# In-place sigmoids in PSUM, and the stores of c11 and p4 on SP's queue, in a one-core decoder layer

## The chip, the cores and the metric

The kernel runs on one core of one Trainium2 chip. The metric is the device time of one execution in microseconds (us); the number to beat or to meet is the median of 3 runs of the kernel before, 2428.19 us (2426.36 to 2428.45). The engines are PE (TensorE, the matmuls), DVE (VectorE), ACT (ScalarE), POOL (GpSimd) and SP (SyncE, which here does nothing but issue DMA transfers). Each engine works through its own list of instructions in a fixed order, and semaphores hold an instruction until what it needs is there.

## The reference

One decoder layer over 2048 tokens of width 1024: a normalised input is projected once to a convolution branch (512 channels, gated, 31 taps) and to eight attention heads of 64; both branches share one output projection; then comes a SwiGLU block. The part that the change touches is the attention, which has no softmax. For a query t and the keys s before it:

```
z = q . k / 8
A[t, s] = sigmoid(z[t, s]) * product over s < j < t of (1 - sigmoid(z[t, j]))
out[t] = sum over s of A[t, s] * v[s]
```

Since 1 - sigmoid(z) = sigmoid(-z), the product is a running product of sigmoid(-z), taken from the newest key back to the oldest. If R[t, s] is the product over j from s to t-1, then A[t, s] = R[t, s+1] - R[t, s], so the kernel never forms A: it multiplies R by differences of neighbouring rows of v (the tile `step`), and adds v once at the end.

## The kernel before, in words

All products run in float32r with both operands split into a high and a low part (H and L): a product is three matmuls, L.H, H.H and H.L, summed in one PSUM bank. ACT makes H by copying with rounding, DVE or POOL makes L by a subtraction.

The work is cut into four groups g of 512 tokens. For each group there are stages on PE, in the order of the table `PLAN`: `in` (input projection, matmuls into `inps`), `mixc` and `outc` (output projection of the convolution half), `mixa` and `outa` (of the attention half), and for the SwiGLU block `fprep`, `c11` and `p4`. The SwiGLU block uses a seven-product scheme in place of eight, on half matrices; `c11` and `p4` are two of its terms that are computed ahead of the rest and kept in DRAM until the later loop `five` reads them. Beside these stages three side tasks run: the attention (`attn`), the convolution taps on DVE (`taps`, L824) and sums of weight halves on POOL (`sums`).

The attention walks over units (head, key chunk of 512). A unit has four `scores`, one for each block of 128 queries, and four `values`. A score is: two matmuls into a PSUM tile `z` (L908, L909), of which there are two; a sigmoid on ACT from `z` into an SBUF tile `om` (L911), of which there are eight; and a scan on DVE, a running product along the keys from right to left. The scan works in place on `om`. There are three forms of it:

- the diagonal chunk (c == g, L914): `lower`, an SBUF tile with a single one per row, is the first input and `om` the second; the widths are 128, 256, 384 and 512 for the four blocks;
- the other chunks (L916): `om` is the first input, and the second, which the operation ignores, is a broadcast of one column, `z[:, 0:1]` in PSUM;
- the same for the last group's heads 4 to 7, where `late` is true: the ignored input is `one`, in SBUF.

So `z` is in use until the sigmoid has read it (diagonal and late scores), or until the scan has finished (the others). `values` then transposes `om` on PE (L934 into `at`), splits it (ACT L590 into `TH`, DVE L591 into `TL`) and multiplies (L939, L940 into `o`).

The results of `c11` (88 tiles of 128 x 512) go from PSUM by ACT (L1146) into four quarters of one SBUF tile, taken in turn, and those of `p4` (22 tiles) by ACT (L1175) into one of four buffers. Each is then stored by `store` (L1109), whose DMA is issued by ACT's own queue (`eng=nc.scalar`, L1147 and L1176; the trace puts the issue at L1111). All other DMAs are issued by SP.

The order of the instructions up to the end of the attention is not the order of the code. A planner inside the kernel (`Graph`, `cost`) takes the recorded instructions, gives each a price, simulates the engines and the buffers, and writes the resulting order on every engine. A DMA costs the queue that issues it 450 ns in that plan; a DVE scan costs 2.04 ns per element and 240 ns more, or 125 ns more where one of its operands lies in PSUM. When the code changes, this plan is made anew.

Of the kernel before, what the change touches and what calls it, by code (L numbers as in the profile page):

```python
# [13 lines left out]
AF = mybir.ActivationFunctionType  # L14
ALU = mybir.AluOpType
# [4 lines left out]
P = 128  # L20
# [5 lines left out]
NH = 8  # L26
# [3 lines left out]
G = 512  # L30
NG = S // G
# [448 lines left out]
def layer_kernel(ctx: ExitStack, tc: tile.TileContext, x, xT, g_pre_mix, w_in, conv_w, conv_b, ln_g, ln_b,  # L480
                 attn_g, w_out, g_post_mix, g_pre_ffn, w_gate, w_up, w_down, g_post_ffn, out):
    nc = tc.nc
# [31 lines left out]
    def bank(name):  # L514
        return mm.tile([P, G], F32, tag="mm", name=name)

    def ev(name, dt=F32, n=G):
        return rp.tile([P, n], dt, tag="ev", name=name, bufs=4)
# [53 lines left out]
    class Weights:  # L572
# [9 lines left out]
        def next(self):  # L582
            while len(self.tiles) < min(self.n + 1 + self.ahead, len(self.srcs)):
                self.tiles.append(self.load(self.srcs[len(self.tiles)]))
            self.n += 1
            return self.tiles[self.n - 1]
# [49 lines left out]
    lower = ap.tile([P, G], F32, name="lower", bufs=1)  # L636
# [5 lines left out]
    one = cc.tile([P, 1], F32, name="one")  # L642
# [3 lines left out]
    for c in range(CB):  # L646
        t = vp.tile([P, PAD + G], F32, name=f"glu{c}")
# [231 lines left out]
    def attn(g):  # L879
# [13 lines left out]
        def fetch(h, c):  # L893
            K = ap.tile([P, G], F32R, tag="K", name="K")
            V = ap.tile([P, G], F32R, tag="V", name="V")
            nc.sync.dma_start(K.bitcast(F32), kd[h, c].bitcast(F32))
            nc.sync.dma_start(V.bitcast(F32), vd[h // 2, c][:, h % 2, :].bitcast(F32))
            return dict(h=h, c=c, K=K, V=V, A=[])

        def scores(u, j):  # L900
            hd_ = heads[u["h"]]
            diag = u["c"] == g
            w = (j + 1) * P if diag else G
            K = u["K"]
            z = pp.tile([P, G], F32, tag="z", name="z")
            late = g == NG - 1 and u["h"] >= NH // 2
            js = slice(j * P, (j + 1) * P)
            nc.tensor.matmul(z[:, 0:w], hd_["QL"][:, js], K[:, 0:w], start=True, stop=False)  # L908
            nc.tensor.matmul(z[:, 0:w], hd_["QH"][:, js], K[:, 0:w], start=False, stop=True)  # L909
            om = ap.tile([P, G], F32, tag="om", name="om", bufs=NOM)  # L910
            nc.scalar.activation(om[:, 0:w], z[:, 0:w], AF.Sigmoid, scale=-0.125)  # L911
            r = om[:, 0:w][:, ::-1]
            if diag:
                nc.vector.tensor_tensor_scan(r, lower[:, G - w:G][:, ::-1], r, hd_["prev"][j], ALU.add, ALU.mult)  # L914
            else:
                nc.vector.tensor_tensor_scan(r, r, (one if late else z[:, 0:1]).to_broadcast([P, w]), hd_["prev"][j],  # L916
                                             ALU.mult, ALU.bypass)
            hd_["prev"][j] = om[:, 0:1]
            if w == P and g:
                hd_["prev"][j] = sp.tile([P, 1], F32, tag="pv", name="pv", bufs=2)  # L920
                nc.gpsimd.tensor_tensor(hd_["prev"][j], om[:, 0:1], lower[:, G - P - 1:G - P], ALU.add)
            u["A"].append(om)
            return w
# [56 lines left out]
        for n in range(len(units) + 1):  # L980
            u = None
            if n < len(units):
                h, c = units[n]
# [3 lines left out]
                u = fetch(h, c)  # L987
            for i in range(TT):
                w = 0
# [11 lines left out]
            if last is not None and last["c"] == 0:  # L1001
                h = last["h"]
                oT = ap.tile([P, G], F32, tag="oT", name="oT", bufs=1)
                nc.scalar.activation(oT, heads[h]["o"], AF.Copy)
                if h % 2 == 0:
                    vsh = ap.tile([P, G], F32, tag="vsh", name="vsh", bufs=1)
                    n = int(g == 0)
# [95 lines left out]
    def matmul(ps, a, b, **flags):  # L1103

        return nc.tensor.matmul(ps, a, b, skip_group_check=True, **flags)  # L1105

    stored = {}

    def store(t, *key, eng=nc.sync):  # L1109
        stored[key] = dp.tile([P, *t.shape[1:]], F32, name="_".join(str(k) for k in key))  # L1110
        eng.dma_start(stored[key], t)  # L1111

    def part(t, k, n, *key, eng=nc.sync):

        if key not in stored:
            stored[key] = dp.tile([P, n, G], F32, name="_".join(str(k) for k in key))
        eng.dma_start(stored[key][:, k, :], t)

    fx = {}

# [9 lines left out]
    def c11(g):  # L1130

        Hs, Ls = fx[g]
        t = cm.tile([P, 2, D], F32, tag="big", name="c11", bufs=2)
        cs = cycle([t[:, i // 2, i % 2 * G:(i % 2 + 1) * G] for i in range(4)])
        wts = Weights([(w, j) for j in range(HF) for w in W], 1)
        for j in range(HF):
            ws = [wts.next() for _ in W]
            pss = [bank("c11") for _ in W]
            for hf in range(2):
                for i, ((WH, WL), ps) in enumerate(zip(ws, pss)):  # L1140
                    for k in range(4):
                        kc = slice((4 * hf + k) * P, (4 * hf + k + 1) * P)
                        for a, b, last in ((WL, Hs, False), (WH, Hs, False), (WH, Ls, k == 3)):
                            matmul(ps, a[:, kc], b[hf][:, k, :], start=hf == k == 0 and a is WL, stop=last)
                    c = next(cs)
                    nc.scalar.activation(c, ps, AF.Copy)  # L1146
                    store(c, "c11", g, i, j, hf, eng=nc.scalar)  # L1147
                    yield 0.5

    def sums_split(HL, k, t, eng=nc.gpsimd):  # L1150
# [4 lines left out]
    def sum_in(g, n, H, L, eng=nc.vector):  # L1155
        for k in range(4):
            t = ev("sumin")
            nc.sync.dma_start(t, stored["B", g, n][:, k, :])
            sums_split((H, L), k, t, eng)

    def p4(g):

        Hs, Ls = ([xp.tile([P, 4, G], F32R, tag=tag, name=tag, bufs=2)] for tag in ("xH", "xL"))
        sum_in(g, 4, Hs[0], Ls[0])
        wts = Weights([(w, j + HF) for j in range(HF) for w in W], load=half_w)
        for j in range(HF):
            for i in range(2):
                WH, WL = wts.next()
                ps = bank("p4")
                for k in range(4):  # L1170
                    kc = slice(k * P, (k + 1) * P)
                    for a, b, last in ((WL, Hs, False), (WH, Hs, False), (WH, Ls, k == 3)):
                        matmul(ps, a[:, kc], b[0][:, k, :], start=k == 0 and a is WL, stop=last)
                c = ev("p4")
                nc.scalar.activation(c, ps, AF.Copy)  # L1175
                store(c, "p4", g, i, j, eng=nc.scalar)  # L1176
                yield 1

    def sums():
# [12 lines left out]
        def flush(n):  # L1192
            while len(late) > n:
                t, kind, *key, m = late.pop(0)
                if kind == "S":
                    ns = (6, 7) if m in (6, 7) else (5, 3)
                    part(t, ns.index(m), 2, kind, *key, ns)
                else:
                    store(t, kind, *key, m)
# [96 lines left out]
    for name, g, cost, *mid in PLAN:  # L1296
# [14 lines left out]
        n = 0  # L1311
# [15 lines left out]
    with ExitStack() as E:  # L1327
# [71 lines left out]
        u = {}  # L1399
# [28 lines left out]
        late = []  # L1428
# [173 lines left out]
        r = [(R[0], f"t{i}") for i in range(4)]  # L1602
# [76 lines left out]
        for i, (g, n, j) in enumerate(slots):  # L1679
# [9 lines left out]
            if n in (5, 3) and j < TT:  # L1689
                T, r = (TB + j, hrows[j]) if n == 5 else (TA + j, hrows[TT + j])  # L1690
# [98 lines left out]
```

## Time and profile before

| | |
|---|---|
| median of 3 runs | 2428.19 us |
| the profiled execution | 2422.51 us, its span 2420.7 us |
| PE busy | 2352.3 us, 97% of the span |
| DVE busy | 1788.4 us, 74% |
| ACT busy | 1166.5 us, 48% |
| POOL busy | 1207.5 us, 50% |
| mean DMA rate | 271 GB/s |
| sigmoids (L911) | 320, from 67.3 to 1364.5 us |
| diagonal scans (L914) | 128, 134.5 us of DVE in four shapes |
| other scans (L916) | 192, of which 48 with `one` |
| stores issued by ACT | 88 of c11, 22 of p4, 256 KB each |

An engine is counted as busy while it executes; a time in which it waits for a semaphore is idle, and the profile names the instruction on another engine that ended it. Times of places are counted from the start of the span. The whole attention lies between 60 and 1385 us; what follows is the loop `five` and the last products.

### The profile page before, as it was taken

The page shows a single profiled execution, that of the slowest core. Times are in us where ns is not written, and L with a number is a line of the kernel's source. Part 1 is how long each engine was busy: PE and PEld are TensorE (multiplying, and loading weights), DVE is VectorE, ACT ScalarE, POOL GpSimd, SP SyncE. Part 2 cuts the span into 40 slices and gives each one's busy share as a digit, 9 for nine tenths or more (in the row PEclk, how much of TensorE's full clock was granted, in tenths as well). Part 3 has the DMA queues.
Part 4 walks back from the last instruction along what each step waited for, and adds up shares of the span by engine and source line. Part 5 has one row for each costly group of instructions (what it writes and reads, how often), then busy time and mean ns, then how long its engine had stood idle before and what let it go on. Part 6 is the DMA issues. An engine that isn't in the chain of part 4 may idle for free. (4 is left out here: it accounts for less than half of the span.)

```text
span 2420.7 us, 33652 instructions
## 1 busy us (share of the span) xinstructions
PE 2352.3 (97%) x11156; PEld 1929.5 (80%) x11156; DVE 1788.4 (74%) x2177; ACT 1166.5 (48%) x2078; POOL 1207.5 (50%) x994
## 2 busy tenths in 40 slices
PE   7999999999999999999999999999999999999997
PEld 5778887788787878888788887878888888887886
DVE  6997899899998799956842267888766664567556
ACT  4346555474655555455555554334322335454543
POOL 5463235522425234436620047678886445477556
PEclk9999999999999999999999999999999999999998
DMA  9889887897788899987798767999998667658664
GB/s 313 273 260 322 260 252 233 275 317 250 249 276 303 272 308 323 332 292 254 261 316 295 255 233 276 309 311 319 348 336 299 198 236 232 199 189 324 193 193 163
DMA packets 283789, 656.66 MB, mean 271 GB/s; under 512 B 34912, under 2 KB 35424, under 8 KB 283616
## 3 DMA queue, kind: packets, MB, share of 16 engines
q1 hardware_dynamic: 267776, 625.68, 77.6%
q10 hardware_dynamic: 15840, 28.84, 3.1%
q8 instruction: 88, 1.44, 0.2%
q14 instruction: 85, 0.70, 0.1%
HBM read 460.40 MB, written 193.99 MB: 270 GB/s over the span
## 5 line engine op out<-in xcount | busy, mean ns | idle before, releaser
L824 DVE SCALAR_TENSOR_TENSOR cv<-glu,cw,cv 128x512 f32<-128x512 f32 x464 | 345.9, 746 | 6.4
L1395 POOL TENSOR_TENSOR wL<-raw,wH 128x512 fp32r<-128x512 f32 x176 | 264.9, 1529 | 169.9 <-ACT wH L1394 169.7
L1625 DVE TENSOR_TENSOR xL__20078<-t__20080,xH__20077 128x512 fp32r<-128x512 f32 x154 | 197.5, 1288 | 150.3 <-ACT xH__20077 L1624 148.9
L1623 POOL TENSOR_TENSOR xL__20076<-t__20079,xH__20075 128x512 fp32r<-128x512 f32 x154 | 212.5, 1385 | 159.4 <-ACT xH__20075 L1622 155.2
L591 DVE TENSOR_TENSOR TL<-at,TH 128x512 fp32r<-128x512 f32 (+1 forms) x320 | 188.6, 597 | 132.8 <-ACT TH L590 126.7
L598 PE MATMUL inps<-xH,wL 128*128 128x512 f32 x640 | 259.7, 407 | 12.4 <-ACT sg L768 11.7
L602 PE MATMUL inps<-xL,wH 128*128 128x512 f32 x640 | 255.3, 400 | 0.5 <-DVE xL L738 0.5
L600 PE MATMUL inps<-xH,wH 128*128 128x512 f32 x640 | 255.7, 400 | 0.0
L1105 PE MATMUL dps<-xH__20075,xL__20078 128*128 128x512 f32 x616 | 241.6, 392 | 5.6 <-DVE xL__20078 L1625 5.6
L1105 PE MATMUL dps<-xH__20075,xH__20077 128*128 128x512 f32 x616 | 240.8, 391 | 0.0
L1105 PE MATMUL dps<-xL__20076,xH__20077 128*128 128x512 f32 x616 | 239.4, 391 | 0.0
L590 ACT ACTIVATE TH<-at 128x512 fp32r<-128x512 f32 (+1 forms) x320 | 168.8, 536 | 122.8 <-PE at L934 114.2
L552 ACT ACTIVATE wH<-raw 128x1024 fp32r<-128x1024 f32 x156 | 165.8, 1063 | 127.6 <-PE inps L602 57.0
L911 ACT ACTIVATE om<-z 128x512 f32<-128x512 f32 (+2 forms) x320 | 168.4, 540 | 88.9 <-PE z L909 87.3
L556 POOL TENSOR_TENSOR wL<-raw,wH 128x1024 fp32r<-128x1024 f32 x50 | 122.1, 2443 | 163.7 <-ACT wH L552 149.4
L934 PE MATMUL at<-idr,om 128*128 128x128 f32 x1088 | 184.2, 273 | 6.0 <-DVE om L914 3.0
L1622 ACT ACTIVATE xH__20075<-t__20079 128x512 fp32r<-128x512 f32 x154 | 97.1, 630 | 192.7 <-POOL xL__20076 L1623 141.5
L1189 POOL TENSOR_TENSOR sum<-sum 128x512 f32<-128x512 f32 x88 | 126.7, 1440 | 117.9 <-DMA sum<-in_w_up_dram 45.0
L1394 ACT ACTIVATE wH<-raw 128x512 fp32r<-128x512 f32 x176 | 101.4, 624 | 155.9 <-PE b L1105 58.3
L934 PEld LDWEIGHTS at<-idr,om 128*128 128x128 f32 x1088 | 137.1, 140 | 46.2 <-DVE om L914 5.8
L916 DVE TENSOR_TENSOR_SCAN om<-om,z 128x512 f32<-128x512 f32 x124 | 156.8, 1268 | 3.9 <-ACT om L911 3.7
L598 PEld LDWEIGHTS inps<-xH,wL 128*128 128x128 f32 x640 | 121.5, 190 | 37.8 <-ACT sg L768 8.3
(296 smaller groups left out, 6120.7 us busy)
## 6 DMA issues: line engine op xcount, KB each, us to landing
wL<-wL SPq DMA_DIRECT2D x156, 512.0 KB, 5.3
raw<-in_w_in_dram SPq DMA_DIRECT2D x80, 512.0 KB, 6.0
t__20080<-u SPq DMA_DIRECT2D x154, 256.0 KB, 3.0
c<-c ACTq DMA_DIRECT2D x88, 256.0 KB, 5.4
t__20079<-wd SPq DMA_DIRECT2D x88, 256.0 KB, 2.6
K<-kd SPq DMA_DIRECT2D x80, 256.0 KB, 4.9
V<-vd SPq DMA_DIRECT2D x80, 256.0 KB, 4.6
u<-accf SPq DMA_DIRECT2D x22, 768.0 KB, 5.7
```

Of the source, the lines that this page charges most:

```text
L590: nc.scalar.activation(H, ps, AF.Copy)
L591: nc.vector.tensor_tensor(L, ps, H.bitcast(F32), ALU.subtract)
L598: nc.tensor.matmul(ps, WL[:, kc], aH[t](k), start=k == 0, stop=False)
L600: nc.tensor.matmul(ps, WH[:, kc], aH[t](k), start=False, stop=False)
L602: nc.tensor.matmul(ps, WH[:, kc], aL[t](k), start=False, stop=k == KT - 1)
L824: nc.vector.scalar_tensor_tensor(to, gl[c][:, k:k + G], cw[:, c, k:k + 1], a, ALU.mult, ALU.add)
L911: nc.scalar.activation(om[:, 0:w], z[:, 0:w], AF.Sigmoid, scale=-0.125)
L934: nc.tensor.transpose(pt[:, j * P:(j + 1) * P], u["A"][j][:, b * P:(b + 1) * P], id32)
L1105: return nc.tensor.matmul(ps, a, b, skip_group_check=True, **flags)
L1395: nc.gpsimd.tensor_tensor(l, t, f32(h), sub)
L1623: nc.gpsimd.tensor_tensor(WL, w, f32(WH), sub)
L1625: nc.vector.tensor_tensor(UL, t, f32(UH), sub)
```

## The change

The sigmoid writes its result back into `z`, in PSUM. The scan reads `z` as the sigmoid's result and writes `om` in SBUF; `om` is no longer written by ACT. The first input of the other chunks' scan is `z`, and the ignored second input is `one` for all heads; the special case `late` is gone. The stores of c11 and p4 are issued by SP like all other DMAs.

```diff
-            late = g == NG - 1 and u["h"] >= NH // 2
...
-            nc.scalar.activation(om[:, 0:w], z[:, 0:w], AF.Sigmoid, scale=-0.125)
-            r = om[:, 0:w][:, ::-1]
+            nc.scalar.activation(z[:, 0:w], z[:, 0:w], AF.Sigmoid, scale=-0.125)
+            r, zr = (t[:, 0:w][:, ::-1] for t in (om, z))
             if diag:
-                nc.vector.tensor_tensor_scan(r, lower[:, G - w:G][:, ::-1], r, hd_["prev"][j], ALU.add, ALU.mult)
+                nc.vector.tensor_tensor_scan(r, lower[:, G - w:G][:, ::-1], zr, hd_["prev"][j], ALU.add, ALU.mult)
             else:
-                nc.vector.tensor_tensor_scan(r, r, (one if late else z[:, 0:1]).to_broadcast([P, w]), hd_["prev"][j],
-                                             ALU.mult, ALU.bypass)
+                nc.vector.tensor_tensor_scan(r, zr, one.to_broadcast([P, w]), hd_["prev"][j], ALU.mult,
+                                             ALU.bypass)
...
-    def store(t, *key, eng=nc.sync):
+    def store(t, *key):
...
-        eng.dma_start(stored[key], t)
+        nc.sync.dma_start(stored[key], t)
...
-                    store(c, "c11", g, i, j, hf, eng=nc.scalar)
+                    store(c, "c11", g, i, j, hf)
...
-                store(c, "p4", g, i, j, eng=nc.scalar)
+                store(c, "p4", g, i, j)
```

Since the plan is made anew, instructions move on every engine between about 45 us and the end of the attention. From there on (the last 4546 of PE's 11158 matmuls) PE's order is the same as before. Lines behind L906 are numbered one lower in the changed kernel. Three places follow; `x5` at a row's end means five equal instructions in a row.

On DVE, in the first group, around the scans of one of the first heads (`cv` and `acc` are convolution taps, `TL` the split of a transposed `om`). Before:

```order
L824 SCALAR_TENSOR_TENSOR cv<-glu_140,cw,cv 128x512 x5
L914 SCALAR_TENSOR_TENSOR om<-lower,om 128x128
L914 SCALAR_TENSOR_TENSOR om<-lower,om 128x256
L914 SCALAR_TENSOR_TENSOR om<-lower,om 128x384
L914 SCALAR_TENSOR_TENSOR om<-lower,om 128x512
L824 SCALAR_TENSOR_TENSOR acc<-glu_140,cw,cv 128x512
L591 TENSOR_TENSOR TL<-at,TH 128x512
```

And now:

```order
L824 SCALAR_TENSOR_TENSOR cv<-glu_140,cw,cv 128x512 x5
L913 SCALAR_TENSOR_TENSOR om<-lower,z 128x128
L824 SCALAR_TENSOR_TENSOR cv<-glu_140,cw,cv 128x512
L913 SCALAR_TENSOR_TENSOR om<-lower,z 128x256
L824 SCALAR_TENSOR_TENSOR cv<-glu_140,cw,cv 128x512
L773 TENSOR_TENSOR glu_142<-inps,sg 128x512
L913 SCALAR_TENSOR_TENSOR om<-lower,z 128x384
L913 SCALAR_TENSOR_TENSOR om<-lower,z 128x512
```

The four scans of a diagonal unit stood together and are now apart, with taps between them; each reads a `z` that is held until then.

On ACT, at the second group's input projection, where the trace of before has its longest wait of PE inside the attention's time (`vt` is the split of v, `sg` the sigmoid of the gate, which empties one of the two banks of `inps`). Before:

```order
L776 ACTIVATE vs<-inps 128x512
L552 ACTIVATE wH<-raw 128x1024
L539 ACTIVATE junk,ss<-big 128x1024
L552 ACTIVATE wH<-raw 128x1024
L960 ACTIVATE sq<-ot 128x512
L590 ACTIVATE vt<-vps 128x4x64 x2
L768 ACTIVATE sg<-inps 128x512
```

And now:

```order
L776 ACTIVATE vs<-inps 128x512
L539 ACTIVATE junk,ss<-big 128x1024
L973 ACTIVATE ma<-po,small_121 128x512
L590 ACTIVATE vt<-vps 128x4x64 x2
L768 ACTIVATE sg<-inps 128x512
```

The two `vt` still stand ahead of `sg`; on DVE, ten taps in a row (x9 and the last, `acc`) stand ahead of the two `vt` there, where before the taps ahead of the first `vt` were broken up (x9, x2, x1).

On SP, at the start of the first `c11` stage, in the changed kernel (`c_0_0_0_0` and its like are stores of c11; `fx` and `B` are stores of operands, `piece` reads them back, `raw` is a weight, K and V are the attention's):

```order
L1110 DMA c_0_0_0_1_9881<-c_9731 128x512
L896 DMA K<-kd_3_215 128x512
L1226 DMA piece<-fx_4_1_9679 128x512
L551 DMA raw<-in_w_up_dram 128x1024
L1110 DMA c_0_1_0_1_9914<-c_9731 128x512
L558 DMA wL_9977<-wL 128x1024
```

The stores of c11 now stand in one line with the loads of K, V and the weights; before, they stood on ACT, each behind its `c<-c`:

```order
L1146 ACTIVATE c_9731<-c_9756 128x512
L1111 DMA c_0_0_0_0_9771<-c_9731 128x512
L1146 ACTIVATE c_9731<-c_9757 128x512
L1111 DMA c_0_1_0_0_9825<-c_9731 128x512
L552 ACTIVATE wH<-raw 128x1024
```

So a store that waited on ACT for the copy just ahead of it now waits on SP, with the loads behind it.

More of the change, by code (lines that the diff above doesn't have):

```diff
@@ L1107, in layer_kernel, with part @@
     stored = {}
-    def store(t, *key, eng=nc.sync):
+    def store(t, *key):
         stored[key] = dp.tile([P, *t.shape[1:]], F32, name="_".join(str(k) for k in key))
-        eng.dma_start(stored[key], t)
-    def part(t, k, n, *key, eng=nc.sync):
+        nc.sync.dma_start(stored[key], t)
+    def part(t, k, n, *key):
         if key not in stored:
             stored[key] = dp.tile([P, n, G], F32, name="_".join(str(k) for k in key))
-        eng.dma_start(stored[key][:, k, :], t)
+        nc.sync.dma_start(stored[key][:, k, :], t)
     fx = {}
```

## The prediction

> **What bounds the kernel now.** I read the head of the page first, then busy time by stretch: to the first attention work, the first group, the groups up to c11, the first c11 and the rest of the attention, and what follows it.
>
> ```profile
> span 2420.7 us, 33652 instructions
> ...
> PE 2352.3 (97%) x11156; PEld 1929.5 (80%) x11156; DVE 1788.4 (74%) x2177; ACT 1166.5 (48%) x2078; POOL 1207.5 (50%) x994
> ...
> 60.00:240.00 180.00, 172.31 (x885) 141.61 (x884) 158.08 (x232) 89.72 (x171) 83.69 (x80) 1.00 0.89 284
> 240.00:880.00 640.00, 623.73 (x3188) 510.38 (x3186) 589.08 (x802) 355.25 (x643) 244.58 (x255) 0.99 0.82 270
> 880.00:1075.00 195.00, 193.74 (x956) 158.85 (x955) 169.60 (x218) 102.10 (x175) 72.28 (x41) 1.00 0.93 325
> 1075.00:1385.00 310.00, 305.45 (x1499) 251.87 (x1498) 159.39 (x175) 170.29 (x298) 107.31 (x88) 0.99 0.81 274
> ```
>
> Behind each stretch's length stand the busy times of PE, PEld, DVE, ACT and POOL, then clock, DMA share and GB/s. PE sets the time, and the matmuls themselves are not changed. From 60 to 1385 us PE is idle for 7.7 + 16.3 + 1.3 + 4.6 = 29.8 us: that is all there is to win. DVE is busy for 88%, 92% and 87% of the first three stretches, so it is the engine that runs late there; ACT is at 50 to 56%.
>
> Third, who ends PE's waits from 60 to 1385 us (sum, times, longest):
>
> ```profile
> PE inps L598 <- ACT sg L768: 7.0, 5, 5.0
> PE o L940 <- DVE TL L591: 4.2, 7, 1.5
> PE o L939 <- ACT TH L590: 3.0, 2, 2.6
> PE at L934 <- DVE om L914: 3.0, 5, 1.0
> PE z L908 <- DVE om L916: 1.9, 5, 0.5
> ...
> PE at L934 <- DVE TL L591: 1.7, 3, 1.1
> ...
> PE at L934 <- ACT ma L974: 0.9, 1, 0.9
> PE z L908 <- ACT om L911: 0.5, 1, 0.5
> ```
>
> These are many short waits on the attention's steps on DVE and ACT, and one of 5.0 us. I count as waits that faster scans can shorten: 4.2 + 1.7 (`TL`, queued behind scans), 3.0 + 1.9 + 0.5 (`om`), 0.9 (`ma`) and 7.0 - 5.0 of `sg`: 14.2 us.
>
> The one of 5.0 us I leave out. Its place in the timeline:
>
> ```profile
> 467.20 0.79 PE L598 MATMUL inps<-xH,wL 128*128 128x512 f32 x1 [5.00 <-ACT sg L768]
> ...
> 466.28 0.38 ACT L590 ACTIVATE vt<-vps 128x256 fp32r<-128x256 f32 x1 [2.13 <-DVE vt L591]
> 466.56 0.59 ACT L768 ACTIVATE sg<-inps 128x512 f32<-128x512 f32 x1
> ...
> 455.55 7.08 DVE L824 SCALAR_TENSOR_TENSOR cv<-glu,cw,cv 128x512 f32<-128x512 f32 x9
> ```
>
> `sg` stands behind the two `vt` on ACT, and these wait for DVE, which works through taps; no scan is near. The new order keeps `vt` ahead of `sg`, and ten taps ahead of both `vt`.
>
> **The scans.** Prices by line and shape (busy us, mean ns), and minimum, median and maximum by line:
>
> ```profile
> L914 DVE TENSOR_TENSOR_SCAN om<-lower,om 128x512 f32<-128x512 f32 x32 | 50.9, 1590 | 2.2 <-ACT om L911 2.2
> ...
> L914 DVE TENSOR_TENSOR_SCAN om<-lower,om 128x384 f32<-128x384 f32 x32 | 39.8, 1244 | 3.1 <-ACT om L911 3.1
> ...
> L914 DVE TENSOR_TENSOR_SCAN om<-lower,om 128x256 f32<-128x256 f32 x32 | 26.2, 817 | 0.8 <-ACT om L911 0.7
> ...
> L914 DVE TENSOR_TENSOR_SCAN om<-lower,om 128x128 f32<-128x128 f32 x32 | 17.6, 551 | 8.6 <-ACT om L911 8.5
> ...
> L916 DVE TENSOR_TENSOR_SCAN om<-om,one 128x512 f32<-128x512 f32 x44 | 64.7, 1481 | 24.9 <-ACT om L911 24.9
> ...
> L916 DVE TENSOR_TENSOR_SCAN om<-om,pv,one 128x512 f32<-128x512 f32 x4 | 5.7, 1430 | 1.6 <-ACT om L911 1.6
> ...
> L914 DVE TENSOR_TENSOR_SCAN om<-lower,om x128: 466/992/3094, 68.0 to 1241.9; 128x128 f32<-128x128 f32 x32, 128x256 f32<-128x256 f32 x32, 128x384 f32<-128x384 f32 x32, 128x512 f32<-128x512 f32 x32
> ...
> L916 DVE TENSOR_TENSOR_SCAN om<-om,z x124: 1241/1269/1284, 228.5 to 1049.1; 128x512 f32<-128x512 f32 x124
> L916 DVE TENSOR_TENSOR_SCAN om<-om,one x44: 1251/1284/2307, 1075.3 to 1365.2; 128x512 f32<-128x512 f32 x44
> ```
>
> The form with `z` in PSUM never leaves 1241 to 1284 ns. The forms with both inputs in SBUF begin at the same price and reach 2307 and 3094 ns: something stretches them, and it spares the form with a PSUM operand. After the change every scan has one. I price them at the `z` form's 1269 for 512 columns and, on the line from there to the 466 of the narrowest, 1001 for 384, 734 for 256 and 466 for 128. Diagonal: 134.5 - 32 x (1.269 + 1.001 + 0.734 + 0.466) = 134.5 - 111.0 = 23.5 us less. Late: 64.7 + 5.7 - 48 x 1.269 = 9.5 us less. The 144 with `z` stay. DVE gets 33.0 us back.
>
> No row has a scan whose first input is in PSUM. The nearest rows bound what that adds: the broadcast from PSUM costs nothing against SBUF's 1251 at the low end, and 1269 - 1251 = 18 ns at the high end, 5.8 us over 320 scans; I take nothing. [...]
>
> Of the 14.2 us of waits I take two thirds back, **9.5 us**: 33.0 us of DVE time is over twice the waits, but it falls where scans are, and some waits come from taps or POOL. Bounds: 0, if these waits only move, and 14.2.
>
> **The sigmoids.** No ACT row writes to PSUM. Nearest are ACT copies of 512 columns from PSUM and from SBUF beside the sigmoid:
>
> ```profile
> L911 ACT ACTIVATE om<-z 128x512 f32<-128x512 f32 x224 | 132.7, 603 | 47.1 <-PE z L909 46.1
> ...
> L1048 ACT ACTIVATE big<-ops 128x512 f32<-128x512 f32 x32 | 18.9, 593 | 19.5 <-PE ops L1043 19.5
> ...
> L1394 ACT ACTIVATE wH<-raw 128x512 fp32r<-128x512 f32 x176 | 101.4, 624 | 155.9 <-PE b L1105 58.3 <-issue 52.2 <-POOL wL L1395 26.7
> ```
>
> Between them lie 31 ns; 320 of these, either way, are 9.9 us of an engine that idles for 46% of its time from 60 to 1385 us. I take 0: ACT's idle time covers it, and without that cover it would be 9.9 us. The wait for a free `om` passes from ACT to DVE; with eight buffers no row shows one.
>
> **The held z.** 176 scores (128 diagonal, 48 late) now keep their `z` until the scan's end. Behind a `z` matmul that waits stands everything on PE. Today 144 scores do so, and PE waited 1.9 us for them. At the same rate: 1.9 x 176 / 144 = **2.3 us lost**. Low end 0, as the new order puts the diagonal scans apart with other work between them; high end: a quarter of the 176 (every fourth score, one for each unit) waiting the mean of today, 1.9 / 5 = 0.38 us, is 16.7 us.
>
> **The stores.** ACT loses 110 issues, SP gains them:
>
> ```profile
> L1111 ACTq DMA_DIRECT2D c<-c x88: 326/326/528, 888.3 to 1383.9; - x88
> L1111 SPq DMA_DIRECT2D u<-accf x51: 319/320/750, 1288.2 to 1996.9; - x51
> ...
> ACT wH L552 <- DMA c<-c: 5.8, 2, 3.7
> ...
> ACT c L1146 <- DMA c<-c: 4.2, 1, 4.2
> ...
> SPq L554 <- PE c L1105: 66.2, 22, 8.1
> ```
>
> 110 x 0.326 = 35.9 us leave ACT's queue, which lies on idle time: nothing for PE. SP takes on 110 x 0.320 = 35.2 us, but it also waits in its line: a store now waits for ACT's copy, and loads of K, V and weights behind it wait too; and a store behind a weight load that waits for PE (22 times, up to 8.1 us) lands later, so that the next copy into its quarter waits longer. Today landings hold ACT for 5.8 + 4.2 = 10.0 us there, which reaches PE hardly at all (1.3 and 4.6 us of idle in these stretches, whatever the cause). Low end 0; high end 10.0, those waits doubled and all passed on to PE. I take **0.5 us lost**, near the low end, as PE has no wait for a DMA in its rows.
>
> **The sum**: -9.5 + 0 + 2.3 + 0.5 = -6.7 us. The profiled execution took 2422.51 us, 1.8 us of them around its span, and would take 2415.8; it lies 5.7 us below the median of the runs, and against that median the forecast is 2428.2 - 6.7 = **2421.5 us**.
>
> **The rivals.** A measurement of this kernel can tell about 0.2%, 4.9 us: faster is below 2423.3, slower above 2433.1.
>
> 1. *Hidden anyway.* PE is at 97%, the plan is new everywhere, and a plan that fits scans better can still leave PE waiting on taps. Then the gain is 2.8 us, the losses cancel it: 2428.2 us. For it: the longest wait has nothing to do with scans. Against: 10.8 us of the waits name `om` or `TL` on DVE.
> [...]
> 3. *The held z becomes the bound*, slower: two `z` tiles, each held for two matmuls, a sigmoid of 0.60 and a scan of 1.27 us. Place: the diagonal units and the last heads. At the high end of 16.7: -9.5 + 16.7 + 0.5 = +7.7, 2435.9 us. It decides from 9.5 - 0.5 = 9.0 us of `z` waits on. For it: PE waits for `om` of L916 already; against: only 5 times in 144.
> 4. *SP becomes the bound in c11*, slower: the DMA share is 0.93 from 880 to 1075 us and 44 stores join SP's line there. It decides once PE shows waits for loads; 22 of SP's waits passed on to PE at a third of their mean of 3.0 us are 22, of which I allow 15 for what PE's order hides: 2436.5 us.
>
> **How the numbers follow.** Forecast 0.55, in its own range of 2416 to 2426 (0.44 below 2423.3, 0.11 above); rival 1: 0.18 (0.16 same, 0.02 slower); rival 2: 0.07 (same); rival 3: 0.12 (0.09 slower, 0.03 same); rival 4: 0.08 (0.06 slower, 0.02 same). Faster 0.44, same 0.39, slower 0.17. The range starts at 2409, where all 14.2 us and the 5.0 us of `sg` are won (-19.2), and ends at 2436, the price of the third rival.
>
> **What will show it.** Right: scans at 1.24 to 1.29 us for 512 columns, diagonal or not, and none of 2 us or more; DVE busy some 33 us less; fewer waits of PE for `om` and `TL`; from 1385 us on the same length. Wrong: `z` waits of 9 us or more; PE waits for DMAs from 880 to 1385 us; scans near 1.33 us; or PE idle for about 30 us from 60 to 1385 us as before, at other places.

## The result, and the profile after

The changed kernel takes 2404.14 us (median of 4 runs, 2402.09 to 2405.29), against 2427.97 us before (2426.36 to 2428.45): a ratio of 0.9902, 95% interval 0.9885 to 0.9919, 23.8 us less. The forecast was 2421.5 us in a range of 2409 to 2436; the direction was right, and the gain is 3.6 times the 6.7 us that were forecast, outside the range.

One part of that difference lies in no trace. The profiled execution of the kernel before took 2422.51 us, 5.5 us below its median, and that of the changed kernel 2405.29 us, 1.2 us above its own. The two traces can therefore account for 17.2 us, not for 23.8.

The head of the page after, and busy time in the same four stretches (length, then PE, PEld, DVE, ACT and POOL, clock, DMA share, GB/s):

```profile
span 2403.5 us, 33872 instructions
...
PE 2350.3 (98%) x11156; PEld 1929.8 (80%) x11156; DVE 1753.6 (73%) x2177; ACT 1164.9 (48%) x2078; POOL 1167.5 (49%) x994
...
60.00:240.00 180.00, 177.17 (x916) 146.74 (x916) 155.96 (x238) 92.90 (x177) 84.45 (x83) 1.00 0.92 296
240.00:880.00 640.00, 627.92 (x3209) 514.57 (x3208) 585.64 (x811) 357.11 (x644) 232.87 (x253) 1.00 0.83 275
880.00:1075.00 195.00, 194.20 (x966) 158.72 (x965) 165.11 (x215) 103.36 (x181) 75.17 (x46) 1.00 0.92 318
1075.00:1385.00 310.00, 309.29 (x1520) 255.57 (x1519) 143.41 (x174) 174.32 (x303) 81.31 (x82) 1.00 0.83 280
```

DVE is busy 1788.4 - 1753.6 = 34.8 us less. PE is idle for 2.8 + 12.1 + 0.8 + 0.7 = 16.4 us from 60 to 1385 us, where it was 29.8: 13.4 us of the 17.2. Of the rest, PE's busy time has 2.0 (2352.3 to 2350.3), and 1.8 were won before 60 us, where no scan had run yet.

The scans, by line and shape (busy us, mean ns), and minimum, median and maximum by line:

```profile
L913 DVE TENSOR_TENSOR_SCAN om<-lower,z 128x512 f32<-128x512 f32 x32 | 40.6, 1269 | 3.6 <-ACT z L910 3.6
L913 DVE TENSOR_TENSOR_SCAN om<-lower,z 128x384 f32<-128x384 f32 x32 | 32.2, 1006 | 4.0 <-ACT z L910 4.0
...
L913 DVE TENSOR_TENSOR_SCAN om<-lower,z 128x256 f32<-128x256 f32 x32 | 23.7, 739 | 1.9 <-ACT z L910 1.7
...
L913 DVE TENSOR_TENSOR_SCAN om<-lower,z 128x128 f32<-128x128 f32 x32 | 15.3, 477 | 15.4 <-ACT z L910 15.4
...
L913 DVE TENSOR_TENSOR_SCAN om<-lower,z x128: 465/869/1282, 64.9 to 1224.5; 128x128 f32<-128x128 f32 x32, 128x256 f32<-128x256 f32 x32, 128x384 f32<-128x384 f32 x32, 128x512 f32<-128x512 f32 x32
...
L915 DVE TENSOR_TENSOR_SCAN om<-z,om,one x168: 1255/1277/1295, 224.0 to 1340.6; 128x512 f32<-128x512 f32 x168
```

The diagonal scans sum to 111.8 us (111.0 forecast, 134.5 before), and no scan is above 1.295 us.

Who ends PE's waits from 60 to 1385 us (sum, times, longest):

```profile
PE ops L1040 <- DVE xL L872: 2.4, 3, 0.9
PE o L939 <- DVE TL L591: 2.2, 4, 0.7
PE z L907 <- DVE om L915: 1.9, 3, 1.0
PE at L933 <- DVE om L915: 1.7, 2, 1.1
PE inps L598 <- ACT sg L768: 1.4, 2, 0.9
PE at L933 <- DVE om L913: 1.4, 1, 1.4
PE at L933 <- ACT ma L973: 0.9, 1, 0.9
...
PE pf L954 <- DVE TL L591: 0.8, 1, 0.8
...
PE o L938 <- ACT TH L590: 0.5, 2, 0.3
```

This list, set against the one in the prediction, is the first sign of which step failed. The waits that the prediction counted (`TL`, `om`, `ma`, and `sg` without its longest) fell from 14.2 to 2.2 + 0.8 + 1.9 + 1.7 + 1.4 + 1.4 + 0.9 = 10.3 us, by 3.9. The two that it left out fell by more: the 5.0 us of `sg` are gone (no wait of that row is longer than 0.9 now), and `TH` went from 3.0 to 0.5.

### The profile page after: what moved, and what is told of

Same layout as the page of the kernel before. It is cut to its first block, busy times and chain, and to the rows that moved or that the text cites. A ratio compares the mean times of both kernels' runs of the same rounds, so it can differ in the third digit from the quotient of the medians.

```text
span 2403.5 us, 33872 instructions
## 1 busy us (share of the span) xinstructions
PE 2350.3 (98%) x11156; PEld 1929.8 (80%) x11156; DVE 1753.6 (73%) x2177; ACT 1164.9 (48%) x2078; POOL 1167.5 (49%) x994
## 5 line engine op out<-in xcount | busy, mean ns | idle before, releaser
L915 DVE TENSOR_TENSOR_SCAN om<-z,om,one 128x512 f32<-128x512 f32 x168 | 214.0, 1277 | 59.3 <-ACT z L910 57.0
L910 ACT ACTIVATE z<-z 128x512 f32<-128x512 f32 (+2 forms) x320 | 167.8, 530 | 112.3 <-PE z L908 103.1
L1188 POOL TENSOR_TENSOR sum<-sum 128x512 f32<-128x512 f32 x88 | 117.2, 1331 | 106.8 <-DMA sum<-in_w_gate_dram 37.9
```

The source lines that it names most:

```text
L915: nc.vector.tensor_tensor_scan(r, zr, one.to_broadcast([P, w]), hd_["prev"][j], ALU.mult, ALU.bypass)
```

## The experiments

Theory A, in the expectations, is that the time follows the DVE time of the scans. The others are that the order drawn anew by the planner decides, whatever the scans cost, or the queue of the stores; each expectation says what it means by its letters. Every kernel was run beside the kernel before on the same chip. Ratios are to that kernel with their 95% intervals, and its median is given in brackets.

### The parts alone

In place for all scores, with the stores left on ACT's queue (e1):

```diff
-            nc.scalar.activation(om[:, 0:w], z[:, 0:w], AF.Sigmoid, scale=-0.125)
+            nc.scalar.activation(z[:, 0:w], z[:, 0:w], AF.Sigmoid, scale=-0.125)
...
-                nc.vector.tensor_tensor_scan(r, lower[:, G - w:G][:, ::-1], r, hd_["prev"][j], ALU.add, ALU.mult)
+                nc.vector.tensor_tensor_scan(r, lower[:, G - w:G][:, ::-1], zr, hd_["prev"][j], ALU.add, ALU.mult)
...
-                nc.vector.tensor_tensor_scan(r, r, (one if late else z[:, 0:1]).to_broadcast([P, w]), hd_["prev"][j],
-                                             ALU.mult, ALU.bypass)
+                nc.vector.tensor_tensor_scan(r, zr, one.to_broadcast([P, w]), hd_["prev"][j], ALU.mult,
+                                             ALU.bypass)
```

> The sigmoids in place, as in the change, but the stores of c11 and p4 stay on ACT's queue. Theory A (the scans are what pays): nearly the whole gain, -17 to -24 us against before. Theory B (the stores are what pays, since a DMA on ACT's queue takes 450 ns of ACT in the plan and holds the copies behind it): -12 us or less of a gain, and the waits of PE between the start of p4 and the second c11 stay near the 9 us of before instead of 2. Theory C (the plan is made anew and its quality is luck): anywhere between -20 and +10 us, with scans as fast as in the change.

Measured: 2412.23 us, 0.9938 [0.9917, 0.9958] (2425.38).

The stores alone (e2):

```diff
-                    store(c, "c11", g, i, j, hf, eng=nc.scalar)
+                    store(c, "c11", g, i, j, hf)
...
-                store(c, "p4", g, i, j, eng=nc.scalar)
+                store(c, "p4", g, i, j)
```

> The kernel before with the stores of c11 and p4 on SP's queue and nothing else changed. Theory A: within 5 us of before, the scans stretched as before (mean 1590 and 1481 ns). Theory B: -5 to -12 us, won from 1075 to 1385 us. Theory C: a change of several us of either sign, also in the first 800 us, where no store stands.

Measured: 2436.24 us, 1.0042 [1.0028, 1.0056]. So the parts alone give -13 and +11 us, and the two together -24: they don't add up, which is what one sees when something besides the parts moves the time. The waits of PE in e2 show where (60 to 1385 us):

```profile
PE o L940 <- DVE TL L591: 11.9, 6, 9.1
PE at L934 <- DVE om L916: 4.9, 6, 1.4
```

The wait of 9.1 us stands at 401.7 us, where no store is issued: it is the plan, made anew, that left a `TL` late there.

The late scores alone (e3), which puts `z` back as the ignored input for heads 4 to 7 of the last group and changes nothing else:

```diff
-            late = g == NG - 1 and u["h"] >= NH // 2
+            late = False
```

> The kernel before without the special case for the last four heads: their scan's ignored input is z in PSUM, not one in SBUF, and z is held until the scan's end. Theory A: the 48 late scans fall from 1481 to 1269 ns, DVE is 9.5 us less busy, and PE gains 0 to 5 us. If the held z costs: PE waits more for om at its z matmuls (1.9 us before), up to 5 us slower. Theory C: a change of either sign that these waits don't explain.

Measured: 2425.6 us, 0.9997 [0.9986, 1.0007]. The late scans fell to 1269 ns as expected, and the time did not move.

The diagonal alone (e4):

```diff
-            nc.scalar.activation(om[:, 0:w], z[:, 0:w], AF.Sigmoid, scale=-0.125)
+            nc.scalar.activation((z if diag else om)[:, 0:w], z[:, 0:w], AF.Sigmoid, scale=-0.125)
...
-                nc.vector.tensor_tensor_scan(r, lower[:, G - w:G][:, ::-1], r, hd_["prev"][j], ALU.add, ALU.mult)
+                nc.vector.tensor_tensor_scan(r, lower[:, G - w:G][:, ::-1], zr, hd_["prev"][j], ALU.add, ALU.mult)
```

> The kernel before with the sigmoid in place in PSUM for the diagonal chunks alone; the other chunks, the late ones and the stores as before. Theory A: the diagonal scans fall to 1.269, 1.00, 0.73 and 0.47 us, DVE is 23.5 us less busy, and two thirds or more of the gain comes with it, -12 to -20 us. Theory B: within 5 us of before. Theory C: a change of either sign.

Measured: 2405.48 us, 0.9912 [0.9896, 0.9928], level with the whole change. Its scans:

```profile
L916 DVE TENSOR_TENSOR_SCAN om<-om,one 128x512 f32<-128x512 f32 x44 | 64.5, 1474 | 57.3 <-ACT om L911 57.3
...
L914 DVE TENSOR_TENSOR_SCAN om<-lower,z 128x512 f32<-128x512 f32 x32 | 40.6, 1270 | 4.6 <-ACT z L911 4.6
```

The late scans are as slow as ever and nothing is lost by it; the diagonal is at 1270 ns, and the gain is there. From these four runs the diagonal looks like the cause, but each of them has an order of its own, and e2 shows that an order can cost 10 us by itself.

### How much an order is worth

To see the size of that, the planner's own prices were nudged by amounts that hardly matter to it, so that it draws another order for the same instructions. In the kernel before: one hop between engines 62 instead of 60 ns (n1), a landing of a DMA 5050 instead of 5000 ns (n2). In the changed kernel: the same two (n3, n4), and 380 ns instead of 450 for issuing a DMA (e11). In e1: the same two (e10, e9).

```diff
-HOP = 60.0
+HOP = 62.0
...
-RATE, ISSUE, AHEAD, LAND = 350.0, 450.0, 700.0, 5000.0
+RATE, ISSUE, AHEAD, LAND = 350.0, 450.0, 700.0, 5050.0
```

> The kernel before with one price of the planner changed by next to nothing (a hop of 62 in place of 60 ns), so that another order of like quality comes out. It measures how far luck of the plan reaches. Theory A: within 5 us of before. Theory C: 5 to 20 us off, either way.

> The changed kernel with the same small change of a planner's price (a hop of 62 ns). Theory A: within 5 us of the changed kernel, so -19 to -29 us against before. Theory C: 5 to 20 us off the changed kernel.

> The kernel before with another small change of the planner's prices (a landing of 5050 in place of 5000 ns). Plans with the slow scans so far: 2424 to 2449 us. Theory A (both hold: fast scans pay, and luck of the plan is worth some 10 us either way): 2420 to 2450 us, above every kernel with fast scans. Theory C alone (luck, no gain of the scans): as likely below 2413 us as above.

> The changed kernel with the same small change of the prices (5050 ns). Theory A: 2400 to 2420 us, below every kernel with slow scans. Theory C alone: as likely above 2424 us as below.

> The sigmoids in place and the stores on ACT, planned with a landing of 5050 ns. Theory D: 2400 to 2420 us, as often below as above the same perturbation with the stores on SP (2403). Theory B: above it by 5 us or more.

> The same with a hop of 62 ns. Theory D: 2400 to 2420 us, as often below as above its pair with the stores on SP (2418). Theory B: above it by 5 us or more.

> The changed kernel, planned with an issue of 380 ns for a DMA in place of 450, nearer to the 320 to 450 ns of the trace. A candidate for a better plan, and one more draw of it. Theory A: 2400 to 2420 us; a price nearer the chip may put it at the low end, 2395 to 2405.

Two more changed what the planner believes of a scan. In p1 the kernel before keeps its real scans, but the planner prices all of them like the fast form; in p2 the changed kernel is planned with the slow price.

```diff
-                b = 2.04 * n + (125 if near else 240)
+                b = 2.04 * n + 125
```

> The kernel before, computing as before; the planner alone is told that every scan costs 2.04 ns per element and 125 ns, also the diagonal and the late ones with both inputs in SBUF. The scans stay slow, the plan takes them for fast. Theory A1 (the DVE time itself pays): no gain, within 6 us of before or slower. Theory A2 (the gain comes from a plan made with the lower price): -10 to -20 us with diagonal scans at 1.45 to 1.6 us as before.

> The changed kernel, computing as the changed one; the planner alone is told that every scan costs 240 ns beside its 2.04 ns per element. The scans are fast, the plan takes them for slower. Theory A1: most of the gain stays, -15 us or more against before. Theory A2: half of it or more is lost, -12 us or less.

The measured times of all kernels with an order of their own, by the form of the diagonal scan that they really run:

| diagonal from SBUF | us | ratio | diagonal from PSUM | us | ratio |
|---|---|---|---|---|---|
| e3 | 2425.6 | 0.9997 [0.9986, 1.0007] | n4 | 2403.27 | 0.9903 [0.9883, 0.9922] |
| before | 2427.97 | 1 | the change | 2404.14 | 0.9902 [0.9885, 0.9919] |
| e2 | 2436.24 | 1.0042 [1.0028, 1.0056] | e4 | 2405.48 | 0.9912 [0.9896, 0.9928] |
| n2 | 2436.94 | 1.0040 [1.0025, 1.0055] | e10 | 2410.9 | 0.9932 [0.9917, 0.9947] |
| n1 | 2443.89 | 1.0086 [1.0071, 1.0101] | e1 | 2412.23 | 0.9938 [0.9917, 0.9958] |
| p1 | 2449.24 | 1.0105 [1.0090, 1.0120] | p2 | 2413.05 | 0.9953 [0.9936, 0.9970] |
| | | | e9 | 2416.64 | 0.9954 [0.9939, 0.9969] |
| | | | n3 | 2417.77 | 0.9970 [0.9956, 0.9984] |
| | | | e11 | 2419.42 | 0.9955 [0.9943, 0.9968] |

Three things follow. A price changed by 1 to 3% moves the time by up to 20 us (n1, against the kernel before on its own chip, 2424.2), so no single pair of planned kernels tells an edit's worth to better than some 10 us. Every kernel of the right side is faster than every one of the left; the means are 2411.4 and 2436.6 us (2434.1 without p1, which is planned with a wrong price), 23 to 25 us apart. And both the kernel before and the change stand near the top of their column, so that the luck of their orders about cancels between them. That the planner merely believes in fast scans brought nothing in the one order that was tried: p1 is the slowest of all.

Several expectations missed. On their own chips e1 gained 13.2 us where theory A had 17 to 24, p2 gained 11.2 where 15 or more were to stay, and e2 lost 10.9 where it was to lie within 5; n1 and n3 moved by more than the 5 us that theory A allowed; e11 is not at the low end of its range. e9 and e10, with the stores on ACT, lie 13 us above and 7 us below the kernels with the same prices and the stores on SP (n4, n3), so that these pairs don't tell what the queue is worth. Against a scatter of this size only runs at a fixed order decide.

### The order held fixed

The last doubt is whether an order in which the diagonal scans take `z` is a better order, apart from their time. Four kernels therefore run exactly the order of the change on every engine.

Two of them add work to DVE that nobody waits for, right behind each of the 128 diagonal scans: a sum over 64 columns of `lower` (e6) or over 256 (e7), out of the planner's sight.

```diff
+MORE = 64
...
+    waste = cc.tile([P, 1], F32, name="waste")
...
+                more = nc.vector.tensor_reduce(waste, lower[:, 0:MORE], AX.X, ALU.add).ins
```

> The changed kernel with exactly its order on every engine; the planner doesn't see that behind each of the 128 diagonal scans DVE also sums 64 columns of a constant tile, a result that nobody reads: about 0.15 us each, 20 us of DVE in all, near the 23.5 us by which these scans were slower before. Theory A (DVE's time is what pays, at a given order): 10 to 25 us slower than the changed kernel, which undoes most of the gain. Theory C (the order decides): within 5 us of the changed kernel.

> The same with sums of 256 columns, about 0.35 us each, 45 us of DVE. Theory A: more than twice the loss of the run with 64 columns, 25 to 60 us slower than the changed kernel. Theory C: within 10 us of it.

Measured: 2414.79 us, 0.9950 [0.9933, 0.9968] and 2432.57 us, 1.0022 [1.0012, 1.0032] (2428.02): 10.7 and 28.4 us above the change. Busy times by engine, the added group and the diagonal scans from first to last start, of e6:

```profile
PE 2361.1 (98%) x11156; PEld 1930.1 (80%) x11156; DVE 1763.2 (73%) x2305; ACT 1166.5 (48%) x2078; POOL 1170.2 (48%) x994
...
L925 DVE TENSOR_REDUCE waste<-lower 128x1 f32<-128x64 f32 x128 | 24.6, 192 | 0.0
...
L924 DVE TENSOR_TENSOR_SCAN om<-lower,z x128: 462/874/1281, 64.8 to 1231.3; 128x128 f32<-128x128 f32 x32, 128x256 f32<-128x256 f32 x32, 128x384 f32<-128x384 f32 x32, 128x512 f32<-128x512 f32 x32
```

And of e7:

```profile
PE 2367.1 (97%) x11156; PEld 1925.5 (79%) x11156; DVE 1794.3 (74%) x2305; ACT 1167.9 (48%) x2078; POOL 1169.6 (48%) x994
...
L925 DVE TENSOR_REDUCE waste<-lower 128x1 f32<-128x256 f32 x128 | 50.3, 393 | 0.0
...
L924 DVE TENSOR_TENSOR_SCAN om<-lower,z x128: 465/872/1281, 63.9 to 1247.7; 128x128 f32<-128x128 f32 x32, 128x256 f32<-128x256 f32 x32, 128x384 f32<-128x384 f32 x32, 128x512 f32<-128x512 f32 x32
```

The records of neighbours on DVE overlap (in e6 the first diagonal scan starts at 64.78 us and lasts 0.48 us, and the sum behind it starts at 65.17), so busy time is the measure: DVE is busy 9.6 us longer in e6 and 40.7 in e7, for 10.7 and 28.4 us of time. Not all of that time comes from the added sums. As PE's order is the change's, the traces can be matched with its trace matmul by matmul: where the attention ends, at 1385 us of the change, e6 is 6.6 us behind and e7 22.9 (the last diagonal scan starts 6.8 and 23.2 us after the change's, which starts at 1224.5). Both lose another 3.8 us between 1600 and 2010 us, long after the last added sum, and with no more waiting than the change. PE gets through fewer matmuls there at the same granted clock, first e6, then the change:

```profile
1700.00:1900.00 200.00, 200.00 (x872) 163.47 (x871) 126.92 (x149) 59.29 (x102) 140.14 (x97) 1.00 0.87 302
...
1700.00:1900.00 200.00, 200.00 (x884) 165.61 (x883) 127.31 (x148) 60.90 (x105) 136.04 (x94) 1.00 0.88 302
```

This slower piece is in the traces of e6 and e7 and in no other; its cause is open. At a fixed order, then, a microsecond of DVE work at these places costs 0.56 us (22.9 for 40.7, e7) to 0.69 us (6.6 for 9.6, e6), though DVE is busy for only 73 to 74% of the span.

The third (e8) issues the stores of c11 and p4 from ACT's queue again, each at the place of ACT's order behind its copy, while the planner goes on reckoning with SP:

```diff
-        nc.sync.dma_start(stored[key], t)
+        eng.dma_start(stored[key], t)
...
-                    store(c, "c11", g, i, j, hf)
+                    store(c, "c11", g, i, j, hf, eng=nc.scalar)
...
-                store(c, "p4", g, i, j)
+                store(c, "p4", g, i, j, eng=nc.scalar)
```

> The changed kernel with exactly its order on every engine, except that the 110 stores of c11 and p4 are taken out of SP's line and issued by ACT at the places that the plan gave them. Theory D (the queue of the stores is worth nothing by itself, and the 8 us between the change and the run with the stores on ACT were luck of the plan): within 4 us of the changed kernel. Theory B (the queue matters): 5 to 10 us slower, between c11's start and the end of the attention.

Measured: 2403.42 us, 0.9900 [0.9885, 0.9914] (2428.39), level with the change. The queue of the stores is worth nothing. SP did take on the waiting that the prediction spoke of, in the profile of the change (sum, times, longest):

```profile
SPq L1110 <- ACT c L1145: 82.6, 61, 3.7
```

Those 82.6 us on SP's queue end in no wait of PE for a DMA from 60 to 1385 us.

The fourth (e12) settles the main question. It is the change with one thing undone: the 128 diagonal sigmoids and scans go through `om` in SBUF again, while the planner sees the change's operands and draws the change's order.

```diff
-            nc.scalar.activation(z[:, 0:w], z[:, 0:w], AF.Sigmoid, scale=-0.125)
+            sg = nc.scalar.activation((om if diag else z)[:, 0:w], z[:, 0:w], AF.Sigmoid, scale=-0.125).ins
...
-                nc.vector.tensor_tensor_scan(r, lower[:, G - w:G][:, ::-1], zr, hd_["prev"][j], ALU.add, ALU.mult)
+                sc = nc.vector.tensor_tensor_scan(r, lower[:, G - w:G][:, ::-1], r, hd_["prev"][j], ALU.add, ALU.mult).ins
```

> Every engine's order is exactly the change's, stores on SP; only the 128 diagonal sigmoids and scans go through om in SBUF again, as in the kernel before (both scan inputs in SBUF). Theory A (the gain is the DVE time of scans that GpSimd stretches, converted at a fixed order): the diagonal scans of 512 columns mean 1450 to 1600 ns again with several over 2 us, DVE is busy 15 to 25 us longer than in the change, and the time is 2415 to 2430 us, 10 to 25 us above the change. Theory C (the gain is the luck of the new order, whatever the scans cost): within 5 us of the change, 2400 to 2409 us.

Measured: 2428.14 us (2427.2 to 2430.36), 1.0011 [1.0001, 1.0020] (2425.7). The whole gain is gone, 24.0 us by the medians and 26 by the ratios to the kernel before, with the order unchanged. Its page, its stretches from 60 to 880 us, its diagonal scans and PE's waits:

```profile
span 2428.1 us, 33803 instructions
...
PE 2357.7 (97%) x11156; PEld 1928.8 (79%) x11156; DVE 1781.3 (73%) x2177; ACT 1166.6 (48%) x2078; POOL 1193.9 (49%) x994
...
60.00:240.00 180.00, 168.16 (x855) 137.99 (x853) 158.32 (x226) 85.08 (x162) 83.77 (x78) 1.00 0.88 278
240.00:880.00 640.00, 624.31 (x3183) 508.36 (x3182) 584.42 (x801) 357.04 (x643) 250.94 (x257) 1.00 0.82 271
...
L917 DVE TENSOR_TENSOR_SCAN om<-lower,om x128: 467/1008/2781, 65.9 to 1247.1; 128x128 f32<-128x128 f32 x32, 128x256 f32<-128x256 f32 x32, 128x384 f32<-128x384 f32 x32, 128x512 f32<-128x512 f32 x32
...
L917 DVE TENSOR_TENSOR_SCAN om<-lower,om 128x128 f32<-128x128 f32 (+3 forms) x128 | 136.6, 1078 | 24.4 <-ACT om L914 24.1
...
PE at L940 <- DVE ot L962: 4.8, 2, 2.5
PE at L940 <- DVE om L917: 4.5, 7, 2.2
PE at L940 <- DVE TL L594: 4.5, 5, 1.2
PE o L946 <- DVE TL L594: 3.3, 6, 0.8
PE z L911 <- DVE om L922: 2.0, 4, 0.7
...
PE inps L601 <- ACT sg L772: 0.6, 1, 0.6
```

DVE is busy 1781.3 - 1753.6 = 27.7 us longer, and the time is 24.0 longer. The last diagonal scan starts at 1247.1 us in place of 1224.5, so 22.6 of the 24.6 us between the two traces are lost before the attention ends. Of these 24.6 us, PE's busy time has 7.4 of the loss (2357.7 against 2350.3) and its idle time the other 17.2. PE is idle for 11.8 + 15.7 us in the two stretches shown, against 2.8 + 12.1 in the change. Of the waits that grew, most name `om` and `TL`, and the largest names `ot`, a reduction on DVE. Two other ways for the loss can be read off: PE's waits that name POOL, which is busy longer here too (1193.9 us against 1167.5), sum to 0.4 us, as in the change, and ACT's sigmoids, which must now find a free `om`, wait 0.4 us for the transposes that free one. The expectation of 1450 to 1600 ns for 512 columns missed: they mean 1375, and the stretching falls on the narrower ones instead (1225 ns for 384 columns, 1016 for 256, 695 for 128); the expected 15 to 25 us of DVE were 27.7.

What stands beside a stretched scan can be seen in two short pieces at the same place of the same order, DVE and POOL from 68 to 76 us (start, duration). The rows of the two engines stand one under the other. First e12, where each DVE row overlaps one of POOL:

```profile
69.42 3.75 DVE L917 TENSOR_TENSOR_SCAN om<-lower,om 128x512 f32<-128x512 f32 x2
...
73.68 2.44 DVE L917 TENSOR_TENSOR_SCAN om<-lower,om 128x256 f32<-128x256 f32 x1
...
70.10 2.80 POOL L559 TENSOR_TENSOR wL<-raw,wH 128x1024 fp32r<-128x1024 f32 x1 [10.29 <-ACT wH L555]
73.18 2.38 POOL L559 TENSOR_TENSOR wL<-raw,wH 128x1024 fp32r<-128x1024 f32 x1 [0.29 <-ACT wH L555]
```

Then the change:

```profile
68.41 1.80 DVE L913 TENSOR_TENSOR_SCAN om<-lower,z 128x512 f32<-128x512 f32 x2
...
71.53 0.74 DVE L913 TENSOR_TENSOR_SCAN om<-lower,z 128x256 f32<-128x256 f32 x1
...
69.04 2.39 POOL L556 TENSOR_TENSOR wL<-raw,wH 128x1024 fp32r<-128x1024 f32 x1 [10.25 <-ACT wH L552]
72.21 2.41 POOL L556 TENSOR_TENSOR wL<-raw,wH 128x1024 fp32r<-128x1024 f32 x1 [0.78 <-ACT wH L552]
```

Two scans (512 and 128 columns) take 3.75 us against 1.80, and one of 256 takes 2.44 against 0.74, beside the same two POOL subtractions (in the change the second overlaps its scan by 0.06 us only, as DVE is ahead by then).

The mirror image, fast scans in the order of the kernel before, was not tried: that order asks for the next `z` ahead of the scan that would free it. No planned kernel beat the change: n4 and e8 tie with it.

## Why the prediction was right, and where it failed

**The scans: right.** 33.0 us of DVE were forecast to come back and 34.8 did, 31.1 of them in the durations of the 320 scans; the forms came out at 1269, 1006, 739 and 477 ns where 1269, 1001, 734 and 466 were priced. For the first input in PSUM the prediction took nothing, bounded by 18 ns: the off-diagonal scans have a median of 1277 ns against 1269 with `z` as the ignored input, 8 ns more, 1.5 us over 192. That such a scan takes near 1.33 us (rival 2, at 0.07), no run shows: the slowest of the change's 320 took 1.295 us.

**What the scans' time is worth: the step that failed.** It is "Of the 14.2 us of waits I take two thirds back, 9.5 us". It sized the gain by the waits whose releaser is a scan or stands directly behind one, and put 33.0 us of DVE time down to 9.5 us of kernel time, a rate of 0.29. At a fixed order, matched matmul by matmul up to the end of the attention, the traces show 22.7 us for 27.7 of DVE (e12), 6.6 for 9.6 (e6) and 22.9 for 40.7 (e7): 0.56 to 0.82, two to three times that rate. Two things were missing. A row of the list of waits names the instruction that came last, and that may be any that stands in DVE's queue: `ot` alone has 4.8 us in e12. And a wait is more than the idle time that the list counts. The record of a matmul of 512 columns lasts 0.39 us, while the next one starts 0.23 us after it (114.14 and 114.37 us in the change), so that up to 0.16 us of each wait stands in PE's busy time. Of the 22.7 us of e12, 16.4 are idle time between records. Of the 6.6 of e6 none is: its matmuls start further apart by too little to leave idle time, and in part they run in two stretches of 3.41 us at a granted clock of 0.50, from 134.9 and 578.6 us, that the change does not have (the mean granted clock is 0.99 in e6 from 60 to 240 us and from 240 to 880, and 1.00 in the change). The number to follow was one that the prediction had read itself: DVE busy for 88 and 92% of the first two stretches.

**The wait of 5.0 us at 462 us: left out for half a good reason.** "No scan is near" holds: in e12, with slow scans, the row of `sg` stands at 0.6 us. It is the new order that removed the wait, though it "keeps `vt` ahead of `sg`, and ten taps ahead of both": what stands near in the order did not tell how late DVE would be there. More time than its length was lost there, which the prediction missed:

```profile
467.00:471.00 4.00, 3.80 (x9) 3.02 (x10) 2.15 (x4) 1.09 (x2) 0.88 (x2) 0.50 0.86 272
...
467.79 0.63 PE L600 MATMUL inps<-xH,wH 128*128 128x512 f32 x1
468.22 0.63 PE L602 MATMUL inps<-xL,wH 128*128 128x512 f32 x1
```

These are the stretch behind that wait in the kernel before and two rows of its timeline: the granted clock is 0.50, and matmuls start 0.43 us apart where 0.23 us is usual, ten times, so 2.0 us more. What lowers the clock, no run shows. In the change it stands at 0.50 from 354.07 to 357.48 us, and in the 3.41 us ahead of that PE was busy for 1.92 us and no wait was longer than 0.86 us.

**"That is all there is to win".** The 29.8 us of idle time were not exceeded, but as a bound they left out PE's busy time, above. The range's lower end, 2409, was built on -19.2 us of named waits, and the time went 5 us below it.

**The late scans: a term with no effect.** Their 9.5 us of DVE time were put in one sum with the diagonal's 23.5. In e3 faster late scans gained nothing, and e4 has nearly the time of the change with slow ones; they lie after 1075 us, where DVE was busy for 159.39 of 310 us. As e3 and e4 have orders of their own, that the late scans are worth nothing is argued; that the diagonal's 128 scans give the whole gain is shown by e12.

**The sigmoids: right at nothing.** They take 595 ns in place of 603.

**The held z: 0, not 2.3 us.** PE waits 1.9 us for `z`, as before, with 320 tiles held in place of 144. The third rival needed 9.0.

**The stores: 0, not 0.5 us.** By e8. SP's queue did wait, 82.6 us for c11's copies, and no PE wait for a DMA came of it; the fourth rival is refuted.

**Hidden anyway, the first rival:** refuted by e12, as the gain goes when the diagonal scans alone are slow again.

**Where luck came in.** The prediction took the new order as neutral and gave its scatter no term, though the plan is made anew everywhere. Between this pair it cancelled (e12 has the change's order and the old time). It need not have: the same edit came out between 2403 and 2419 us.

## What to carry to other kernels

When one engine is nearly full over a stage and the bounding engine waits for it in many small pieces, price an edit by the time that it takes from the full engine in that stage, at a rate that a run at a fixed order gives (here 0.56 to 0.82), and not by the waits that name the edited instruction; the name is only the next in the queue. Where a planner draws the order anew, the effect of an edit is read at a fixed order or over several plans, since a pair of plans can differ by 10 us or more for no reason of the edit (n1 lies 19.7 us above the kernel before). And a scan on DVE with both inputs in SBUF, beside a busy POOL, is worth trying with one input in PSUM: here, at a fixed order, that took the mean of the diagonal's 512 columns from 1375 to 1269 ns and the kernel from 2428.14 to 2404.14 us (e12 and the change); other operations of two tensors were not tried.

## What the runs showed of the hardware

In the kernel before and in e12, no scan with both inputs in SBUF was stretched without POOL at work beside it. Counted over the records, with 6% above the usual duration as the mark: before, 29 of 128 diagonal scans and 14 of 48 late ones, up to 3094 ns, and all 43 overlap a POOL instruction; in e12, 30 of 128, again all of them beside POOL. Not every scan beside POOL is: 43 of 93 are before, and 30 of 67 in e12. With one operand in PSUM none is: 0 of 320 in the change, of which 167 ran beside POOL. POOL's time goes the same way: a sum of weight halves means 1440 ns before, 1331 after and 1372 in e12. Its rows before and after:

```profile
L1189 POOL TENSOR_TENSOR sum<-sum 128x512 f32<-128x512 f32 x88 | 126.7, 1440 | 117.9 <-DMA sum<-in_w_up_dram 45.0 <-DMA sum<-in_w_gate_dram 43.3 <-issue 18.3
```

```profile
L1188 POOL TENSOR_TENSOR sum<-sum 128x512 f32<-128x512 f32 x88 | 117.2, 1331 | 106.8 <-DMA sum<-in_w_gate_dram 37.9 <-DMA sum<-in_w_up_dram 35.6 <-issue 19.2
```

POOL is busy 1207.5 - 1167.5 = 40.0 us less; at the same order, e12 against the change, the difference is 1193.9 - 1167.5 = 26.4 us. No run shows why about half of the scans beside POOL are spared, nor why the others are stretched; what was not expected is that one scan of 128 columns would take 2431 ns (e12, at 70.75 us) where 477 is usual.
